# Another order of the units in the rounds of the RWKV-7 scan

## The chip, the core and the metric

The kernel runs on one core of a Trainium2 chip. The metric is the device time of one execution in microseconds (us), the median of the runs. A core has a matrix engine (TensorE, PE in the profile; PEld is its weight load), a vector engine (VectorE, DVE), a scalar engine (ScalarE, ACT), a general engine (GpSimd, POOL) and a queue engine (SyncE, SP) from which this kernel issues its DMA transfers. Each engine works through its own instructions in the order in which they stand in the program; between engines they wait on semaphores. Matrix products accumulate in PSUM, all other tiles lie in SBUF.

## The reference, cut to what matters

The program is a backbone of four layers over 256 latent and 256 context tokens of width 1024: attention, RWKV-7 time mixing, pooling, attention, each followed by a squared-ReLU MLP. All is float32. The change lies in layer 1, in the recurrent scan, which runs in two directions over 16 heads of width 64, first over the context and then, from the state reached there, over the latent tokens:

```
def _wkv_scan(state0, r, decay, k, v, kk, a, reverse):
    xs = tuple(jnp.moveaxis(t.astype(jnp.float32), 1, 0) for t in (r, decay, k, v, kk, a))

    def step(state, inp):
        r_t, w_t, k_t, v_t, kk_t, a_t = inp
        sa = jnp.einsum("bhvk,bhk->bhv", state, kk_t)
        state = (state * w_t[:, :, None, :]
                 - sa[..., None] * (kk_t * a_t)[:, :, None, :]
                 + v_t[..., None] * k_t[:, :, None, :])
        return state, jnp.einsum("bhvk,bhk->bhv", state, r_t)

    state, ys = lax.scan(step, state0, xs, reverse=reverse)
    return state, jnp.moveaxis(ys, 0, 1)
```

## The kernel before

The scan is done in chunks of 64 tokens. Within a chunk, the recurrence is a triangular system: its matrix (L, from the Gram products of keys and decays) is inverted, and the outputs and the chunk's effect on the state are then matrix products. The work is cut into 16 *units*, one for each block of 128 channels (two heads, `cc` 0 to 7) and stream (`s` = 1 context, 0 latent). One unit holds four chunks, two directions and two heads. A unit passes through stages, each written as a Python generator that issues a step of the stage's instructions each time it is called:

- `a` (`front_a`, lines 938 to 979): decays, keys and rates of the unit; ScalarE's E and iL, VectorE's tw, cum and ta. Its first step holds the product of line 943 and kkn (line 945).
- `b` (`front_b`, 981 to 1006): first step the Gram inputs KB and AR (988, 990 on VectorE, 989, 991 on GpSimd), then two steps of Gram products (996) with their masks NG (1001), whose L is stored to DRAM (1003), last the load of its diagonal blocks N (1006).
- `z` (`base`, 1051 to 1088): inversion of the 16x16 diagonal blocks on VectorE, in five steps: three of small products and subtractions (1067, 1069; two, two and three pairs), one with 1074 to 1076, one with 1078 to 1080, which also sends the result through DRAM into the tiles XT and X (1084, 1087).
- `c` (`front_c`, 1008 to 1047): six steps; the third and the fourth are transposes of KB with the copy NG (1035, 1037).
- `k` (`mv`, 1093 to 1102): M V, the product of the masked Gram matrix and V (1098), copied to XR (1101).
- `l` (`levels`, 1104 to 1137): two levels that grow the inverse from 16 to 64. Four steps: product L X and Tm (1114, 1126); two products and the subtractions into XT and X (1114, 1134, 1136); product L X and Tm on ScalarE (1114, 1128); product and subtraction into XT (1134).
- `h` (`chunks`, 1139 to 1183): five steps; two with line 1147, the third with the products 1157 and the subtractions P and Rp (1163, 1164), the fourth 1171, the fifth 1180 and Q (1182).
- `x` (`chain`, 1185 to 1214): the state S from chunk to chunk. `f` (`finish_a`) and `g` (`norms`, with `gate`, 1255 to 1264): normalization, gate and output of a finished block.

The matrix products of `k`, `l` and `h` write PSUM tiles `inv`, of which there are two; a third one waits until the first has been read. The transposes and Gram products share two tiles `pre`.

The units are pipelined: round n issues steps of different units at once. Which unit a letter works on is n plus its entry in `AHEAD` (`l` and `k`, `h`: the next unit, `z` and `c`: two ahead, `b`: three), and the order of the letters in the second string of `STEPS` is the order of the steps in a round. This order is binding for TensorE and VectorE alone: `ordered` chains their instructions one behind the other. For ScalarE, GpSimd and the DMA queue a scheduler orders the instructions by its own estimate.

The 16 rounds come in three kinds, and the text calls them so. In *even* rounds n the chain starts a new block (context), in *odd* ones it works on the latent stream. In *gate* rounds, n = 4, 8 and 12, which are even, two finished blocks are normalized and gated on top (`G`; lines 1233 to 1263).

Of the kernel before, what the change touches and what calls it, by code (L numbers as in the profile page):

```python
# [20 lines left out]
class Kern:  # L21
# [1337 lines left out]
AHEAD = dict(l=1, k=1, x=0, z=2, c=2, f=0, h=1, b=3, a=4, g=0, G=-1, A=3)  # L1359
STEPS = [[(z, AHEAD[z]) for z in order.split()] for order in (  # L1360
    "k l l l l z z z z z c c c c c c h h h h h A A b b b b a a",
    "G x c c x x c x x l x c l z k x G l A c A l x f c z z G h h b f a z G h z h h b G G f b b a g")]

ORDERED = 0
IN_ORDER = (mybir.EngineType.PE, mybir.EngineType.DVE)
# [162 lines left out]
```

## Time and profile before

| | us |
|---|---|
| median of 3 runs | 2509.22 (2504.28 to 2515.09) |
| profiled execution | 2503.11 |
| its span | 2501.3 |
| PE busy | 2324.9 (93%) |
| DVE busy | 1697.7 (68%) |
| ACT busy | 1110.1 (44%) |
| POOL busy | 324.9 (13%) |

The shares are averages over the whole program, most of which is MLP and projections. The scan's rounds lie between about 850 and 1320 us. In the profile a row of the timeline gives start and duration of one group of like instructions, and in brackets how long the engine stood idle before it and what it waited for.

### The profile page before, as it was taken

Reading aid. Unit: us, or ns where it says so; the run is one execution under the profiler, and the core shown is the slowest. Engines: PE = TensorE matmul, PEld = TensorE weight load, DVE = VectorE, ACT = ScalarE, POOL = GpSimd, SP = SyncE. Lnnn points to the kernel's source line nnn. Section 1 sums busy time; section 2 is a strip of 40 time slices with the busy share of each in tenths; the row PEclk is TensorE's granted clock in tenths of the full one; section 3 lists DMA queues with packets and bytes.
Section 4 is the critical chain, followed back from the end, with each engine's and each line's share of the span. In section 5 each row is a group of like instructions: output and inputs, shape, how many; then the busy total and the mean of one; then the engine's idle time right before and its main releaser. Section 6 shows DMA issues by size and latency. Waiting matters only on the chain. (4 is left out here: it accounts for less than half of the span.)

```text
span 2501.3 us, 41970 instructions
## 1 busy us (share of the span) xinstructions
PE 2324.9 (93%) x17082; PEld 1872.4 (75%) x17082; DVE 1697.7 (68%) x2845; ACT 1110.1 (44%) x2038; POOL 324.9 (13%) x414
## 2 busy tenths in 40 slices
PE   7999999999899987787889999999999999988999
PEld 5556888888677766565667888887888888866999
DVE  5777786673786566766666868655786673787555
ACT  4678523323564334443434532333523323576443
POOL 0100011101201222222210101110111100110110
PEclk9999999999899999999999999999999999998999
DMA  7431354553122322211132455532155452103453
GB/s 281 179 116 35 126 202 168 201 187 117 70 85 88 87 45 43 41 37 37 34 68 97 152 186 187 194 141 101 68 203 193 176 202 90 68 26 110 169 186 135
DMA packets 154833, 308.32 MB, mean 123 GB/s; under 512 B 107152, under 2 KB 111632, under 8 KB 122768
## 3 DMA queue, kind: packets, MB, share of 16 engines
q1 hardware_dynamic: 154640, 305.65, 35.8%
q8 instruction: 134, 2.20, 0.3%
q14 instruction: 59, 0.48, 0.1%
HBM read 294.58 MB, written 11.03 MB: 122 GB/s over the span
## 5 line engine op out<-in xcount | busy, mean ns | idle before, releaser
L252 DVE TENSOR_TENSOR wL<-wraw,wH 128x1024 fp32r<-128x1024 f32 (+1 forms) x364 | 408.2, 1124 | 288.1 <-ACT wH L251 287.5
L251 ACT CAST wH<-wraw 128x1024 fp32r<-128x1024 f32 (+1 forms) x364 | 342.1, 943 | 455.4 <-PE mm L262 432.3
L262 PE MATMUL mm<-hH,wL 128*128 128x512 f32 (+1 forms) x1296 | 471.4, 364 | 3.7 <-DVE wL L252 3.6
L262 PE MATMUL mm<-hH,wH 128*128 128x512 f32 (+1 forms) x1296 | 471.5, 364 | 2.6 <-ACT wH L251 2.4
L262 PE MATMUL mm<-hL,wH 128*128 128x512 f32 (+1 forms) x1296 | 466.5, 360 | 0.0
L262 PE MATMUL mm<-uH,wH 128*128 128x512 f32 (+1 forms) x1072 | 380.6, 355 | 0.0
L262 PE MATMUL mm<-uL,wH 128*128 128x512 f32 (+1 forms) x1072 | 379.4, 355 | 0.4 <-DVE uL L398 0.2
L262 PE MATMUL mm<-uH,wL 128*128 128x512 f32 (+1 forms) x1072 | 379.5, 354 | 0.0
L202 DVE SCALAR_TENSOR_TENSOR acc<-wraw,sc_sb,acc 128x2048 f32<-128x2048 f32 x126 | 300.4, 2404 | 25.1 <-DMA wraw<-in_w_mod 19.6
L394 POOL TENSOR_TENSOR usq<-relu 128x512 f32<-128x512 f32 (+1 forms) x128 | 146.3, 1144 | 1239.6 <-ACT relu L392 1237.1
L262 PEld LDWEIGHTS mm<-hH,wH 128*128 128x128 f32 x1296 | 245.4, 189 | 56.3 <-ACT wH L251 12.3
L262 PEld LDWEIGHTS mm<-hH,wL 128*128 128x128 f32 x1296 | 245.7, 190 | 43.8 <-DVE wL L252 6.2
L262 PEld LDWEIGHTS mm<-hL,wH 128*128 128x128 f32 x1296 | 245.6, 190 | 36.6 <-issue 1.1
L262 PEld LDWEIGHTS mm<-uL,wH 128*128 128x128 f32 x1072 | 202.3, 189 | 29.3 <-DVE uL L398 1.2
L262 PEld LDWEIGHTS mm<-uH,wL 128*128 128x128 f32 x1072 | 202.7, 189 | 28.4
L262 PEld LDWEIGHTS mm<-uH,wH 128*128 128x128 f32 x1072 | 202.7, 189 | 28.1
L341 DVE SCALAR_TENSOR_TENSOR x<-mm,mod,x 128x256 f32<-128x256 f32 x272 | 122.0, 479 | 146.1 <-PE mm L262 146.0
L392 ACT ACTIVATE relu<-mm 128x512 f32<-128x512 f32 (+1 forms) x128 | 69.2, 544 | 283.1 <-PE mm L262 279.4
L273 PE MATMUL mm<-hH,wH 128*128 128x256 f32 (+1 forms) x248 | 79.4, 323 | 17.5 <-ACT hH L323 10.0
L397 ACT CAST uH<-usq 128x512 fp32r<-128x512 f32 (+1 forms) x128 | 72.5, 568 | 47.9 <-POOL usq L394 47.9
L398 DVE TENSOR_TENSOR uL<-usq,uH 128x512 fp32r<-128x512 f32 (+1 forms) x128 | 80.5, 630 | 10.4 <-ACT uH L397 9.5
L273 PE MATMUL mm<-hH,wL 128*128 128x256 f32 (+1 forms) x248 | 78.1, 317 | 3.4 <-DVE wL L252 3.4
(344 smaller groups left out, 3697.1 us busy)
## 6 DMA issues: line engine op xcount, KB each, us to landing
wraw<-in_w_mod SPq DMA_DIRECT2D x96, 1024.0 KB, 4.9
wraw<-in_w_in SPq DMA_DIRECT2D x64, 1024.0 KB, 5.9
wraw<-in_w_out SPq DMA_DIRECT2D x64, 1024.0 KB, 5.0
wraw<-in_w_qk SPq DMA_DIRECT2D x10, 1024.0 KB, 4.8
wraw<-in_w_rkv SPq DMA_DIRECT2D x9, 1024.0 KB, 4.8
wraw<-in_w_ao SPq DMA_DIRECT2D x16, 512.0 KB, 4.0
Ls<-NG SPq DMA_DIRECT2D x32, 128.0 KB, 2.7
XT<-Xs SPq DMA_DIRECT2D x32, 128.0 KB, 3.1
```

Source lines behind the costliest of these rows:

```text
L202: nc.vector.scalar_tensor_tensor(acc, raw, self.sc[:, k, s:s + 1], acc, op0=ALU.mult, op1=ALU.add)
L251: nc.scalar.copy(h[:, sl], raw[:, sl])
L252: nc.vector.tensor_sub(l[:, sl], raw[:, sl], h[:, sl].bitcast(F32))
L262: self.nc.tensor.matmul(ps, lhsT=a[:, k], rhs=b, start=(n == 0), stop=(n == 3 * nk - 1))
L273: self.nc.tensor.matmul(ps[:, lo:hi], lhsT=a[:, k], rhs=b, start=(k == z == 0), stop=(k == nk - 1 and z == 2))
L341: self.nc.vector.scalar_tensor_tensor(self.x[o][:, a:b], ps, G[:, o, s:s + 1], self.x[o][:, a:b], op0=ALU.mult, op1=ALU.add)
L392: nc.scalar.activation(r[:, :n], ps[:, :n], AF.Relu)
L394: nc.gpsimd.tensor_mul(u2[:, :n], r[:, :n], r[:, :n])
L397: nc.scalar.copy(uH[:, :n], u2[:, :n])
L398: nc.vector.tensor_sub(uL[:, :n], u2[:, :n], uH[:, :n].bitcast(F32))
```

## The change

Only the string of a round in `STEPS` is another. The same steps are issued for the same units, in another order:

```
 AHEAD = dict(l=1, k=1, x=0, z=2, c=2, f=0, h=1, b=3, a=4, g=0, G=-1, A=3)
 STEPS = [[(z, AHEAD[z]) for z in order.split()] for order in (
     "k l l l l z z z z z c c c c c c h h h h h A A b b b b a a",
-    "G x c c x x c x x l x c l z k x G l A c A l x f c z z G h h b f a z G h z h h b G G f b b a g")]
+    "G x c c x x c x x c l x k l z z x G l A c A l x f c z z G h h f G h b a h z h b G G f b b a g")]
```

TensorE, the first half of a round, here an even one (`inv<-X,NG` is the first product of a level, `inv<-XT,Tm_6465` and `inv<-Tm_6465,XT` the second pair, `pre<-c_base,KB` the KB transposes, `inv<-VU,NG` is M V):

```order
 L1211 MATMUL yps<-Rp,S 64x64 x4
 L1201 MATMUL chain<-S,P 64x64 x4
+L1035 MATMUL pre<-c_base,KB 128x128 x4
 L1114 MATMUL inv<-X,NG 64x64 x16
 L1211 MATMUL yps<-Rp,S 64x64 x4
-L1035 MATMUL pre<-c_base,KB 128x128 x4
+L1098 MATMUL inv<-VU,NG 64x64 x16
 L1114 MATMUL inv<-XT,Tm_6465 64x64 x16
 L1114 MATMUL inv<-Tm_6465,XT 64x64 x16
-L1098 MATMUL inv<-VU,NG 64x64 x16
 L1201 MATMUL chain<-S,P 64x64 x4
```

The KB transposes move ahead of the first level product, and M V comes between the first product and the second pair.

VectorE, behind the subtractions of the first level in an even round (the rows of lines 1067 and 1069 are inversion steps; S and tw follow):

```order
 L1067 TENSOR_TENSOR tb<-Nb,Zb 64x24
 L1069 TENSOR_TENSOR Zb<-Zb,tb 64x2x6x2
+L1067 TENSOR_TENSOR tb<-Nb,Zb 64x30
+L1069 TENSOR_TENSOR Zb<-Zb,tb 64x2x5x3
+L1067 TENSOR_TENSOR tb<-Nb,Zb 64x32
+L1069 TENSOR_TENSOR Zb<-Zb,tb 64x2x4x4
 L1206 SCALAR_TENSOR_TENSOR S<-chain,lam,Q 128x64 x2
 L960 TENSOR_SCALAR tw<-tw 128x512
```

Two more pairs of the inversion's second step now stand in front of S; they are taken out of a place behind the second XT subtraction and line 1047, where the three pairs of the third step stay.

VectorE, further on in the same round (P and Rp of the `h` stage; KB, AR are Gram inputs, kkn belongs to the `a` stage; 1078 is the last inversion step):

```order
 L1163 TENSOR_TENSOR P<-c_rwkvB,inv 128x256
 L1164 TENSOR_TENSOR Rp<-AR,inv 128x256
+L988 TENSOR_TENSOR KB<-ta,iL 128x4x64
+L990 TENSOR_TENSOR AR<-kkn,E 128x4x64
+L988 TENSOR_TENSOR KB<-ta,iL 128x4x64
+L990 TENSOR_TENSOR AR<-kkn,E 128x4x64
+L945 SCALAR_TENSOR_TENSOR kkn<-kvr,vecs_sb,pre 128x256
 L1078 TENSOR_TENSOR tb<-Zb,tc 64x512
 L1079 TENSOR_REDUCE Zb<-tb 64x8x8
```

KB, AR and kkn stood ahead of line 1074 and now stand behind P and Rp, in front of the last inversion step. On TensorE, the product of line 943 moves behind that of line 1157.

On the engines that the scheduler orders, two things are different in a round: in odd rounds ScalarE has Tm (1128) and XR (1043) ahead of E (966), as it already had in even ones, and GpSimd has ks (1015) ahead of KB (989). The DMA queue keeps its order but for gate rounds, where the store of the first half of L (1003) now stands ahead of the reads of XT and X (1087).

## Rows read from the trace of the kernel before

**Rows 1.** The page of the kernel before: its first line, span and instructions.

```profile
span 2501.3 us, 41970 instructions
```

**Rows 2.** Waits, 850:1320 us: total us, times, longest.

```profile
PE inv L1180 <- DVE Rp L1164: 40.4, 13, 5.8
```

**Rows 3.** Stretches, odd and even round: busy us by engine, then granted clock, DMA.

```profile
1033.00:1061.00 28.00, 22.32 (x440) 17.93 (x438) 18.55 (x51) 11.62 (x29) 6.86 (x13) 1.00 0.22 42
...
1061.00:1090.00 29.00, 24.14 (x449) 19.71 (x445) 19.95 (x53) 10.94 (x27) 6.73 (x12) 0.94 0.20 38
```

**Rows 4.** Timeline of TensorE, an even round: start us, duration us; idle before.

```profile
1060.78 1.15 PE L1114 MATMUL inv<-X,NG 64*64 64x64 f32 x32 [0.64 <-DMA X<-Xs]
...
1062.09 0.66 PE L1035 MATMUL pre<-c_base,KB 128*128 128x128 f32 x4
...
1062.68 1.15 PE L1114 MATMUL inv<-XT,Tm 64*64 64x64 f32 x32
...
1065.29 0.97 PE L1098 MATMUL inv<-VU,NG 64*64 64x64 f32 x26 [0.52 <-DVE XT L1134]
...
1078.56 1.95 PE L1180 MATMUL inv<-VU,NG 128*64 128x64 f32 x32 [3.05 <-DVE Rp L1164]
```

**Rows 5.** Timeline of VectorE, the same even round.

```profile
1066.57 0.48 DVE L1206 SCALAR_TENSOR_TENSOR S<-chain,lam,Q 128x64 f32<-128x64 f32 x2 [0.20 <-PE chain L1201]
...
1069.20 0.42 DVE L1134 TENSOR_TENSOR XT<-XT,inv 128x256 f32<-128x256 f32 x1
...
1070.84 0.17 DVE L1067 TENSOR_TENSOR tb<-Nb,Zb 64x30 f32<-64x30 f32 x1
...
1073.05 0.18 DVE L1067 TENSOR_TENSOR tb<-Nb,Zb 64x30 f32<-64x30 f32 x1
...
1074.20 0.41 DVE L988 TENSOR_TENSOR KB<-ta,iL 128x256 f32<-128x256 f32 x1
...
1076.12 0.20 DVE L1074 COPY Zb<-Zb 64x64 f32<-64x64 f32 x1
...
1079.00 0.68 DVE L1078 TENSOR_TENSOR tb<-Zb,tc 64x512 f32<-64x512 f32 x1
...
1080.72 0.68 DVE L1182 TENSOR_TENSOR Q<-inv,lam 128x512 f32<-128x512 f32 x1
...
1082.38 1.29 DVE L1001 TENSOR_TENSOR NG<-pre,c_rwkvB 128x512 f32<-128x512 f32 x2 [0.99 <-PE pre L996]
```

**Rows 6.** Timeline of GpSimd, the same even round.

```profile
1070.86 1.43 POOL L989 TENSOR_TENSOR KB<-key,iL 128x256 f32<-128x256 f32 x2
...
1072.25 0.72 POOL L1015 TENSOR_TENSOR ks<-key 128x256 f32<-128x256 f32 x1
```

**Rows 7.** Timeline of the DMA queue (SPq), the same even round: issues.

```profile
1086.13 1.30 SPq L1087 DMA_DIRECT2D X<-Xs  x2
```

**Rows 8.** Timeline of TensorE, the odd round behind it.

```profile
1090.00 1.15 PE L1114 MATMUL inv<-X,NG 64*64 64x64 f32 x32 [0.64 <-DMA X<-Xs]
...
1098.21 1.15 PE L1114 MATMUL inv<-XT,Tm 64*64 64x64 f32 x32 [1.21 <-ACT Tm L1128]
...
1107.63 1.15 PE L1180 MATMUL inv<-VU,NG 128*64 128x64 f32 x32 [1.93 <-DVE Rp L1164]
```

**Rows 9.** Timeline of VectorE, the same odd round.

```profile
1099.40 0.42 DVE L1134 TENSOR_TENSOR XT<-XT,inv 128x256 f32<-128x256 f32 x1 [1.69 <-PE inv L1114]
```

**Rows 10.** Timeline of TensorE, a gate round.

```profile
994.61 0.66 PE L1035 MATMUL pre<-c_base,KB 128*128 128x128 f32 x4 [2.01 <-ACT ta L956]
...
1017.06 1.98 PE L1180 MATMUL inv<-VU,NG 128*64 128x64 f32 x32 [5.75 <-DVE Rp L1164]
```

**Rows 11.** Timeline of VectorE, the same gate round.

```profile
1017.50 0.89 DVE L1078 TENSOR_TENSOR tb<-Zb,tc 64x512 f32<-64x512 f32 x1
...
1023.72 0.69 DVE L1260 TENSOR_TENSOR yc<-yc,ssum 128x512 f32<-128x512 f32 x1 [1.51 <-ACT ssum L1259]
```

**Rows 12.** Timeline of GpSimd, the same gate round.

```profile
1016.58 2.95 POOL L1251 TENSOR_TENSOR yc<-yc,kvr 128x512 f32<-128x512 f32 x2 [3.43 <-ACT yc L1250]
```

More of the change, by code (lines that the diff above doesn't have):

```diff
@@ L1361 @@
     "k l l l l z z z z z c c c c c c h h h h h A A b b b b a a",
-    "G x c c x x c x x l x c l z k x G l A c A l x f c z z G h h b f a z G h z h h b G G f b b a g")]
+    "G x c c x x c x x c l x k l z z x G l A c A l x f c z z G h h f G h b a h z h b G G f b b a g")]
 ORDERED = 0
```

## The prediction

> **What bounds the kernel now.** I read the page first for the span, then the waits of the stretch in which the change works (the recurrent scan, about 850 to 1320 us), and then the timeline of its engines, iteration by iteration. The profiled execution took 2503.11 us for a span of 2501.3 us [rows 1], so 1.8 us lie around the span; the median of the runs shown is 2509.22 us, 6.1 us above that execution. Sums below are made against the profiled execution, and the difference is then set against the median.
>
> The scan is a loop of 16 rounds of some 28 us. Three kinds come in turn: even rounds, odd rounds, and every fourth round a gate round (even, with the output gate of a finished pair of chunks). In the waits the largest stop of TensorE is the product of line 1180, which waits for the R subtraction on VectorE: 40.4 us in 13 rounds [rows 2]. By the timelines these are 4 even rounds with 3.05 us, 6 odd ones with 1.93 and 3 gate rounds with 5.2 to 5.8; one of each is shown [rows 4, 8, 10]. What goes on meanwhile is seen in the VectorE rows of an even round [rows 5]: from the second XT subtraction (1069.20) to Q (1080.72) it works nearly without a stop. TensorE waits, but VectorE is what it waits for. So a wait on TensorE that goes is only worth what VectorE then does earlier for the next round.
>
> What carries a round into the next is a loop: Gram mask NG on VectorE, which ends at 1083.67 [rows 5]; behind it on the DMA queue the reads of X [rows 7]; these land 6.3 us after the mask, and the first level product of the next round waits for them, at 1090.00 with 0.64 us idle [rows 8], at 1060.78 the same [rows 4]. I therefore follow one number per round: when the first NG mask starts, counted from the first level product. Gate rounds have another entry and a longer tail, see below.
>
> **The change, part by part (even round, first level product at 1060.78).**
> 1. *M V ahead of the second level product, KB transposes ahead of the first.* Before, the product ran 1.31 us with the yps products behind it, then the KB transposes 0.59 (1062.09 to 1062.68), then the second level pair [rows 4]. After, M V (0.97) stands there in place of the transposes: the pair starts 0.39 later, and so does the XT subtraction behind it. M V's old place (0.52 wait and 0.97 work) becomes a wait for the X subtraction, of about the same length, so nothing is lost or won there. The transposes now fill the DMA wait in front of the first product: 0.59 into 0.3 to 1.3 us. I take 0.1 lost on average, between 0 and 0.3.
> 2. *Two more inversion steps (four small VectorE instructions) behind the level subtractions.* Before, they ran from 1070.84 to 1073.05, 2.21 us, beside GpSimd's KB and ks work (1070.86 to 1072.97); six like them right behind took 1.15 us with GpSimd done [rows 5, 6]. In the new place GpSimd has no such work in this round, and I take 4 x 0.20 = 0.80. They delay what follows: S (which no longer waits its 0.20), tw, cum, ta and the second XT subtraction. That comes at 1069.20 + 0.39 + 0.80 - 0.20 = 1070.2, 1.0 later, and E on ScalarE, GpSimd's AR and KB, and the yf addition are as late.
> 3. *What then falls beside GpSimd.* The next six inversion instructions start at 1071.9. GpSimd, as late as E, is then at ks (0.72, now ahead of KB) and KB (1.43) and done at about 1074.1 [rows 6]. I take three of the six stretched to the ends of GpSimd's pieces and three at full speed: done at 1074.75, 0.55 later than before (1074.20).
> 4. *P and R in front of the Gram inputs.* Four KB and AR products and kkn, 1.92 us (1074.20 to 1076.12) move behind P and R [rows 5]. R comes 1.92 - 0.55 = 1.4 earlier, and line 1180 waits 1.7 instead of 3.05. In the trace the product after the long wait took 1.95 us, against 1.15 in an odd round after a wait of 1.93 [rows 4, 8], and the mean granted clock of the even round is 0.94 where that of an odd one is 1.00 [rows 3]. With a wait no longer than the odd one's I expect the 2.4 GHz level to be kept. The Gram product then follows line 1180 with at most 0.2 for KB and AR.
> 5. *The sum on VectorE.* From the end of the six small ones to Q it is the same set of instructions, 6.52 us (1074.20 to 1080.72), in another order: Q starts 0.55 later. But then 0.99 us of wait for the Gram product goes [rows 5]. NG: 0.55 - 0.99 = -0.44. With the 0.1 of part 1, -0.35 per even round. Ends: -1.0 if the six small ones are not stretched at all, +0.1 if all are held to GpSimd's end.
>
> *Odd round after an even one.* The parts are the same. In addition ScalarE now runs the Tm product ahead of E, so the 1.21 us wait of the last level product goes [rows 8]; VectorE idled 1.69 us before the second XT subtraction [rows 9], which hides parts 1 and 2 (0.39 + 0.80) and leaves it 0.5 earlier. Against that stand three stretched small instructions where there was one, and no wait before NG to win back. I take 0; -0.5 to +0.6.
>
> *Gate round.* Here the first product starts on another path: ScalarE's table load and the work behind it, for which TensorE waits 2.01 us [rows 10]. That work starts behind the yvar product, which in the odd round before follows line 1180 and so moves up by about 1.3; half of this, 0.7, reaches the first level product, with the KB transposes done before it. The second XT subtraction comes 0.3 later (+0.39 + 0.80 - 0.20 - 0.7). The small instructions end 0.8 earlier: 2.2 of them have left this place, two of the six that stay are stretched by some 0.55 each. P and R come 0.8 + 1.92 = 2.7 earlier, and line 1180, which waits 5.75 us and then takes 1.98 [rows 10], with them. Q and NG gain less, about 1.1, since KB, AR and kkn stand ahead of them now. But the gate behind NG waits 1.51 us for TensorE's gate product [rows 11], which follows line 1180, so that this wait goes too: 1.1 + 1.5 = 2.6. What may be lost: GpSimd's two yc additions, 2.95 us [rows 12], now run beside KB and AR. I take -2.5 for the round, between -4 and -0.5.
>
> *Odd round after a gate one.* There is no DMA wait before the first product, so the transposes' 0.59 is paid in full: +0.6, between 0 and +1.
>
> Sum: even 4 x -0.35 = -1.4; odd 4 x 0; gate 3 x -2.5 = -7.5; odd after gate 3 x +0.6 = +1.8: -7 us. All the low ends give -18, all the high ends +4.
>
> How much two engines hinder each other is the disputed size. The row shows a VectorE instruction beside GpSimd's yc addition with 0.89 us [rows 11] and, without it, 0.68 in an even round [rows 5]: stretched, not stopped for the 1.47 of an addition. The Trainium skill ("SBUF — State Buffer", Who interferes with whom) says that a VectorE instruction with two SBUF inputs and a GpSimd one that reads SBUF exclude each other for the whole instruction, whoever starts first. By that rule the KB and AR products of the gate round would stand still until the additions end. The trace agrees with it in the even round, where the small instructions end with GpSimd's pieces, and not in the 0.89.
>
> **The rivals.**
> - *KB and AR held up in the gate round.* Both additions (2.95 us, [rows 12]) must end before the second of the four products runs: 1.0 more in each of 3 rounds: -7 + 3 = -4 us, 2505. For it: the small instructions of the even round end where GpSimd's pieces end. Against: the 0.89. This is the result of the rule quoted above.
> - *TensorE is the bound.* Then the wait before line 1180 is the price itself: 6 x 1.2, 4 x 1.4 and 3 x 2.5 less, and as much again from the low clock and from the 1.21 us: about -26 us, 2483. For it: 40.4 us of wait in one place. Against: VectorE works through the same stretch.
> - *Slower: the Gram inputs become the last.* KB and AR stand behind P and R now. If the Gram product must wait for the whole 1.92 us of them, the 0.99 us before NG stays, so the 0.55 of part 3 is paid, and with it the 0.59 of the transposes where ScalarE's VU copies free their buffer too late for the DMA wait: 1.1 us in 12 rounds, +13 us, 2522. It decides from the point where line 996 waits over 1 us for VectorE. For it: in the trace KB and AR were always done long before the product. Against: line 1180 itself, at its 1.15 us, covers the first two of the four (0.41 each).
> - *No change of the period.* X's landing stays where it is, because the queue of small transfers and not NG sets it: 0, 2509. Against: the read of X is issued right behind NG's store.
>
> **How the numbers follow.** Forecast -7 us: 2509.2 - 7 = 2502 us, chance 0.5. Gate products held up (2505) 0.13, TensorE the bound (2483) 0.15, slower (2522) 0.12, no change 0.10. About 0.5%, 12.5 us, is what a measurement of this kernel can tell from no change. Faster by more: the TensorE rival and the forecast's low end (0.18 of its 0.5): 0.33. Slower: 0.13. Between: 0.54. Range: from 2487, near the TensorE case and below the sum of the low ends, to 2514, the high ends and the scatter of the runs shown (2504 to 2515).
>
> **What would show it.** Right: in even rounds line 1180 waits about 1.7 us and runs 1.15 us, the wait before NG is gone, the small instructions behind kvr are still stretched, those behind X are not; odd rounds lose the 1.21 us wait and keep their length; gate rounds are 2 to 3 us shorter. Wrong: line 996 waits for KB or AR; the first level product waits for ScalarE; even rounds shorter by over 1 us (then VectorE was not the bound); gate rounds as long as before.

## The result and the profile after

The changed kernel takes 2522.98 us (median of 8 runs, 2520.22 to 2531.84) beside 2509.64 of the kernel before: the ratio is 1.0059, 95% interval 1.0041 to 1.0077. It is slower, by 13 us in the medians and 15 by the ratio; the forecast was 7 us faster. Its profiled execution took 2520.22 us; the page gives its span:

```profile
span 2518.4 us, 41974 instructions
```

The span is 17.1 us longer than before [rows 1]. The profiled execution of before lies 6.5 us below its median and that of the changed kernel 2.8, so a difference between these two traces comes out some 4 us too large. In the table, a round is counted from one first Tm subtraction (line 1126) to the next; each row is worked out from the 15 starts of one trace. *Plain* rounds are those which are neither gate rounds nor directly ahead of one.

| us | 8 plain rounds, mean | 3 rounds ahead of a gate round, sum | gate rounds 4, 8, 12 | all 14 |
|---|---|---|---|---|
| before | 28.03 | 85.8 | 37.4, 37.4, 36.7 | 421.5 |
| after | 29.33 | 89.4 | 38.4, 38.2, 41.0 | 441.7 |

The scan carries all of it: +20.2 us. The granted clock of TensorE (the third figure from the right in these windows, which give us busy by engine) fell over its whole length, from 0.96 before to 0.89 after:

```profile
850.00:1320.00 470.00, 376.92 (x6845) 299.32 (x6845) 312.50 (x805) 193.86 (x434) 106.33 (x182) 0.96 0.22 42
```

```profile
850.00:1320.00 470.00, 391.18 (x6509) 300.85 (x6509) 313.38 (x791) 191.26 (x422) 105.52 (x181) 0.89 0.21 41
```

The waits of TensorE in it (as in [rows 2]: total us, times, longest):

```profile
PE pre L996 <- DVE NG L1001: 23.8, 10, 2.4
PE inv L1147 <- DVE XT L1134: 15.1, 14, 3.2
...
PE pre L996 <- DVE AR L990: 6.2, 13, 1.5
...
PE inv L1180 <- DVE Rp L1164: 5.1, 6, 2.8
```

The 40.4 us in front of line 1180 have shrunk to 5.1. In their place stands a wait in front of the *second* Gram product of a unit, 2.38 us in 10 rounds: it needs the two `pre` tiles that the first product filled, and so the first NG mask. TensorE in round 6, the even round that [rows 4] show of before:

```profile
1070.97 1.15 PE L1114 MATMUL inv<-X,NG 64*64 64x64 f32 x32
...
1086.82 1.15 PE L1180 MATMUL inv<-VU,NG 128*64 128x64 f32 x32 [0.21 <-DVE Rp L1164]
1088.15 1.16 PE L996 MATMUL pre<-AR,KB 64*128 64x128 f32 x16 [0.18 <-DVE AR L990]
1089.24 0.70 PE L1228 MATMUL pre<-yf,c_base 128*128 128x256 f32 x2
1092.32 1.55 PE L996 MATMUL pre<-AR,KB 64*128 64x128 f32 x15 [2.38 <-DVE NG L1001]
...
1099.27 1.11 PE L1035 MATMUL pre<-c_base,KB 128*128 128x128 f32 x4
...
1101.90 1.15 PE L1114 MATMUL inv<-X,NG 64*64 64x64 f32 x32
```

The KB transposes ahead of the last row take 1.11 us, against 0.66 before [rows 4]. The windows of this round say why:

```profile
1071.00:1092.00 21.00, 16.61 (x373) 13.69 (x372) 16.12 (x43) 7.22 (x17) 5.31 (x9) 1.00 0.06 10
...
1094.00:1102.00 8.00, 7.64 (x61) 5.48 (x62) 2.92 (x9) 4.44 (x10) 1.48 (x4) 0.57 0.54 107
```

In the 8 us behind the new wait TensorE stands at its 1.2 GHz level for most of the time and is busy in 7.64 us of 8. The same round of the kernel before:

```profile
1078.00:1083.00 5.00, 4.42 (x50) 3.81 (x50) 3.94 (x10) 0.00 (x0) 0.00 (x0) 0.66 0.20 21
1083.00:1090.00 7.00, 5.73 (x73) 4.18 (x73) 3.78 (x11) 4.11 (x11) 1.78 (x4) 1.00 0.55 118
```

There the low clock lay on line 1180 and the first Gram product, and the way to the next first level product ran at 1.00. VectorE in round 6 after, to be held against [rows 5]:

```profile
1079.95 0.41 DVE L1134 TENSOR_TENSOR XT<-XT,inv 128x256 f32<-128x256 f32 x1
...
1083.09 0.64 DVE L1067 TENSOR_TENSOR tb<-Nb,Zb 64x24 f32<-64x24 f32 x1
...
1084.38 0.20 DVE L1074 COPY Zb<-Zb 64x64 f32<-64x64 f32 x1
...
1087.26 0.41 DVE L988 TENSOR_TENSOR KB<-ta,iL 128x256 f32<-128x256 f32 x1
...
1090.90 0.67 DVE L1182 TENSOR_TENSOR Q<-inv,lam 128x512 f32<-128x512 f32 x1
1091.50 1.27 DVE L1001 TENSOR_TENSOR NG<-pre,c_rwkvB 128x512 f32<-128x512 f32 x2
...
1097.30 0.48 DVE L1206 SCALAR_TENSOR_TENSOR S<-chain,lam,Q 128x64 f32<-128x64 f32 x2 [2.20 <-PE chain L1201]
```

The first mask starts 20.53 us behind the first level product (1070.97 to 1091.50), where it was 21.60 (1060.78 to 1082.38): 1.07 earlier. From the mask to the next first level product it is 10.40 us instead of 7.62: 2.78 later. That is the loss of this round, 1.71 us, and it lies behind the point to which the prediction counted.

### The profile page after: what moved, and what is told of

It reads as the page before. It is cut to its first block, busy times and chain, and to the rows that moved or that the text cites. A ratio compares the mean times of both kernels' runs of the same rounds, so it can differ in the third digit from the quotient of the medians.

```text
span 2518.4 us, 41974 instructions
## 1 busy us (share of the span) xinstructions
PE 2351.2 (93%) x17082; PEld 1885.1 (75%) x17082; DVE 1704.1 (68%) x2845; ACT 1112.7 (44%) x2038; POOL 325.4 (13%) x414
## 5 line engine op out<-in xcount | busy, mean ns | idle before, releaser
L996 PE MATMUL pre<-AR,KB 64*128 64x128 f32 x512 | 51.9, 325 | 34.1 <-DVE NG L1001 23.8
```

The source lines that it names most:

```text
L996: self.in_turn([nc.tensor.matmul(flat(pg[hh][:, q]), lhsT=flat(KB[rows(hh), dd, q]), rhs=AR[rows(hh), q, :, g(dd)], start=True, stop=True) ...
```

## Experiments

Two theories. **T1**: the 2.38 us gap lets TensorE fall to 1.2 GHz, and the slow stretch now lies on the entry of the next round, where TensorE is the bound. **T2**: VectorE's new order makes the second Gram product late, and the clock is a bystander. The strings below are the part of the round that differs; "..." stands for what is equal.

**The parts alone.** Transposes and M V alone:

```
-... c c x x c x x l x c l z k x G ...
+... c c x x c x x c l x k l z x G ...
```

> Only the KB transposes ahead of the first level product and M V between the level products; inversion steps and P, R stay where they were. Theory T1 (a gap of 2.4 us between the two Gram products lets TensorE fall to the 1.2 GHz level, and the slow stretch then lies on the entry of the next round): no such gap arises here, the second Gram product waits 0.2 to 0.3 us as before, 2509 us within 4. Theory T2 (KB, AR, kkn and the last inversion step in VectorE's order delay the second Gram product, and the clock is a bystander): the same, 2509. Rival T3 (the transposes and M V, not the P and R subtractions, carry the loss): 2520 us, with the first level product waiting for nothing and later by 0.6 to 1 us in each round.

Measured: 2514.51 us, ratio 1.0020 (1.0006 to 1.0033), 1.5 us above the range of T1 and T2. No new wait between the Gram products. The plain rounds are as before (28.28 on average); the rounds ahead of a gate round and the gate rounds are longer (96.6 and 117.3 in sum, against 85.8 and 111.4). A small loss, half of what T3 wanted.

The inversion's second step alone:

```
-... l x c l z k x G ...   f c z z G h h b f a z G h z h h b ...
+... l x c l z z k x G ... f c z G h h b f a z G h z h h b ...
```

> Only the inversion's second step moved behind the first level's subtractions. T1 and T2: P and R come up to 1.4 us earlier, the wait of line 1180 falls from 3.05 to about 2 us in even rounds, no new gap between the Gram products (0.2 to 0.3 us): 2503 to 2509 us. T3: the same.

Measured: 2507.16 us, ratio 0.9987 (0.9971 to 1.0002); the wait of line 1180 falls to at most 2.7 us. As expected.

P and R in front of the Gram inputs alone:

```
-... f c z z G h h b f a z G h z h h b ...
+... f c z z G h h f z G h b a h z h b ...
```

> Only P and R in front of KB, AR and kkn (the inversion's steps at their old places). T1 and T2: the second Gram product waits 2 to 2.5 us for the NG mask as in the changed kernel, and the kernel is slower than before, 2516 to 2524 us; by T1 with a granted clock of 0.5 in the 6 to 10 us behind that wait. T3: no loss, 2509 us or less.

Measured: 2526.03 us, ratio 1.0064 (1.0049 to 1.0079), the whole loss and 2 us more than the expected range. Its trace has the wait and the low clock behind it (TensorE, then a window):

```profile
1095.32 2.37 PE L996 MATMUL pre<-AR,KB 64*128 64x128 f32 x15 [2.38 <-DVE NG L1001]
...
1102.99 1.11 PE L1035 MATMUL pre<-c_base,KB 128*128 128x128 f32 x4
```

```profile
1094.00:1104.00 10.00, 8.68 (x56) 6.32 (x56) 4.40 (x10) 3.14 (x8) 1.29 (x3) 0.55 0.49 93
```

Both theories allow that; the next ones tell them apart.

**The gap filled.** The changed kernel, with the first Gram product issued three times over:

```
-  for q in range(4) for hh in range(2)])
+  for q in range(4) for hh in range(2) for _ in range((FILLER, 1)[dd])])
...
+FILLER = 3
```

> The changed kernel with the first Gram product of each unit issued three times over (the same values written again), so that TensorE works through the 2.38 us in which it waited for the NG mask; VectorE's order and work are the same. T1: the granted clock stays near 1.00 through the second Gram product and the entry of the next round, the first level product comes 2 to 3 us earlier behind the mask, and 10 rounds give back 15 to 25 us: 2498 to 2508 us. T2: the mask is no earlier and the added products are in the way: 2523 to 2530 us.

Measured: 2517.48 us, ratio 1.0020 (1.0004 to 1.0036), outside both ranges. The plain rounds do what T1 says, 27.32 us on average. Round 6:

```profile
1069.43 1.15 PE L1114 MATMUL inv<-X,NG 64*64 64x64 f32 x32 [0.33 <-DMA X<-Xs]
...
1086.23 3.25 PE L996 MATMUL pre<-AR,KB 64*128 64x128 f32 x48 [0.18 <-DVE AR L990]
...
1090.40 1.55 PE L996 MATMUL pre<-AR,KB 64*128 64x128 f32 x15 [0.30 <-DVE NG L1001]
...
1097.06 1.15 PE L1114 MATMUL inv<-X,NG 64*64 64x64 f32 x32
```

```profile
1092.00:1098.00 6.00, 5.64 (x93) 4.28 (x92) 3.00 (x9) 4.55 (x11) 1.91 (x5) 1.00 0.61 134
```

VectorE's order is that of the changed kernel, TensorE has 2.1 us more to do, the clock stays at 1.00, and the entry takes 6.66 us from the second Gram product (1090.40) instead of 9.58 (1092.32 to 1101.90). But in gate rounds the gate's own products stand in the gap and the filler lies on the path: those take 41.6, 43.4 and 42.8 us. Hence the same without rounds 4, 8 and 12 (the line added there makes the line numbers behind it one higher, as in the other runs that add lines):

```
+  for _ in range(1 if dd or self.it in (4, 8, 12) else 3)])
```

> The changed kernel with the first Gram product issued three times over, but not in rounds 4, 8 and 12, where the products of the gate already stand between the two Gram products and the added ones lay on the path (4.87 us at a granted clock of 0.5 in the run with the filler in all rounds). T1: rounds 1 to 3, 6, 7, 10 and 11 at 27.6 us as with the filler in all rounds, gate rounds as in the changed kernel: 2517.5 less 3 x 3 to 4 us, 2503 to 2509. T2: 2515 to 2523.

Measured: 2512.39 us, ratio 1.0005 (0.9992 to 1.0017): against 1.0059 the filler gives back 0.54%, 13.6 us, nearly the whole loss. T2 is out. The time is 3 us above T1's range: gate rounds take 119.4 us in sum and the rounds ahead of them 91.9, against 117.7 and 89.4 in the changed kernel. Round 8 takes 42.8 us without filler of its own, so the filler was not all that made it long.

A second trace of the changed kernel, from the runs side by side below, says the same without any filler. Its rounds 5 and 6 both have the gap; then TensorE:

```profile
1062.10 2.36 PE L996 MATMUL pre<-AR,KB 64*128 64x128 f32 x15 [2.38 <-DVE NG L1001]
...
1071.86 1.15 PE L1114 MATMUL inv<-X,NG 64*64 64x64 f32 x32
...
1093.05 1.55 PE L996 MATMUL pre<-AR,KB 64*128 64x128 f32 x15 [2.38 <-DVE NG L1001]
...
1099.73 1.15 PE L1114 MATMUL inv<-X,NG 64*64 64x64 f32 x32
```

```profile
1064.00:1072.00 8.00, 8.00 (x54) 5.29 (x52) 2.63 (x7) 4.48 (x11) 1.86 (x4) 0.51 0.65 130
1095.00:1101.00 6.00, 5.71 (x106) 4.60 (x108) 2.72 (x10) 4.68 (x11) 1.78 (x4) 1.00 0.57 126
```

In round 5 the clock falls behind the gap and the entry takes 9.76 us, in round 6 it holds and the entry takes 6.68; the rounds take 30.45 and 27.88. In the first trace it is the other way round: 27.27 and 30.93. So the low clock costs about 3 us where it falls, and the gap by itself does not.

**The mask earlier instead.** In the changed kernel, the last inversion step behind the first mask:

```
-... h h f G h b a h z h b G G ...
+... h h f G h b a h h b z G G ...
```

> The changed kernel with the last inversion step (lines 1078 to 1080, 1.7 us on VectorE) behind the first NG mask instead of ahead of P's Gram stage; nothing is added. The mask comes 1.7 us earlier, so that the second Gram product waits 0.2 to 0.8 us instead of 2.38; the results of the inversion go out through DRAM 2 us later against the mask and the first level product waits for X again. T1: the clock is kept, the round is set by X: 2505 to 2516 us, with most of the low-clock stretches behind line 996 gone. T2: the mask is what sets the round, so the whole 1.7 us come back in 10 rounds: 2500 to 2507 us.

Measured: 2527.22 us, ratio 1.0063 (1.0049 to 1.0078); both ranges missed. The gap shrinks to at most 0.9 us (0.68 ahead of the row below), but X, which that step sends through DRAM, becomes the last, and the clock falls on its wait instead:

```profile
PE inv L1114 <- DMA X<-Xs: 20.6, 10, 3.6
```

```profile
1109.99 1.98 PE L1114 MATMUL inv<-X,NG 64*64 64x64 f32 x32 [3.10 <-DMA X<-Xs]
```

**Was the low clock free before?** The kernel before with filler ahead of line 1180, in even rounds without a gate:

```
-  for q in range(4) for hh in range(2) for dd in range(2)])
+  for q in range(4) for hh in range(2) for dd in range(2)
+  for _ in range(1 if self.it % 2 or self.it in (4, 8, 12) else 3)])
```

> The kernel before with the product of line 1157 issued three times over in even rounds without a gate, 2.6 us of TensorE work ahead of the 3.05 us in which line 1180 waits for VectorE. T1 in the form that the low clock costs nothing where VectorE is what TensorE waits for: the clock stays near 1.00 around line 1180 in those rounds, and the time stays within 3 us of before, 2506 to 2512. If low clock cost the same wherever it falls: 4 to 5 rounds times 1 to 2 us less, 2500 to 2504 us.

Measured: 2508.20 us, ratio 0.9990 (0.9977 to 1.0002), in the range for "costs nothing". Round 6 of its trace (line 1180 is 1181 here):

```profile
1064.88 1.15 PE L1114 MATMUL inv<-X,NG 64*64 64x64 f32 x32 [0.45 <-DMA X<-Xs]
...
1083.10 1.10 PE L1181 MATMUL inv<-VU,NG 128*64 128x64 f32 x32
...
1092.84 1.15 PE L1114 MATMUL inv<-X,NG 64*64 64x64 f32 x32 [0.28 <-DMA X<-Xs]
```

It takes 27.96 us against 29.22 before (1060.78 to 1090.00). But that is the round that gained most: the four with filler (0, 2, 6, 10) take 28.68, 28.03, 27.96 and 28.90 us, before 28.39, 27.80, 29.22 and 29.47, 1.3 us less in sum. So the low clock cost little at the old place, against some 3 us a round at the new one; whether by its place or by its length (0.66 over 5 us before, 0.57 over 8 after) no run tells apart.

**Without the transposes and M V.** Inversion steps and P, R moved, the rest as before, without filler and with it outside gate rounds:

```
-... c c x x c x x c l x k l z z x G ...
+... c c x x c x x l x c l z z k x G ...
```

> The change without its first part: inversion steps and P, R moved, KB transposes and M V where they stood in the kernel before, no filler. T1: the wait of 2.4 us between the Gram products and the low clock behind it are there, so that it lies 8 to 14 us above the same order with the filler: 2514 to 2522 us. T2: the filler cannot matter in this order either: 2507 within 3.

> The filler outside gate rounds as above, and of the change only the inversion steps and the P and R subtractions; the KB transposes and M V stand where they stood in the kernel before. The run with the transposes and M V alone was 5 us slower than before. T1 with that part as a loss of its own: 2500 to 2506 us, below both kernels. T2: 2512 to 2523.

Measured: 2514.55 us, ratio 1.0007 (0.9997 to 1.0018), and with filler 2506.75 us, 0.9985 (0.9972 to 0.9999). The second beats both kernels, by a hair against before, and lies 0.75 us above T1's range; its plain rounds take 27.17 us. The filler is worth 0.22% here, less than the 8 to 14 us that T1 wanted, though the trace has 24.6 us of the gap's wait in 11 rounds. The traces show a part of the reason: with the filler the 14 rounds take 417.0 us instead of 440.9, but round 0 begins at 887.0 us instead of 878.2. The filler also stands in the three units whose Gram products come ahead of round 0; that it costs the time there was not tested.

**The change without P and R** (`h h b f a G h z h h b` in place of `h h f G h b a h z h b`):

> The change without P and R in front of the Gram inputs: transposes, M V and inversion steps moved. Both theories hold the P and R subtractions for the cause of the gap: no wait over 1 us between the Gram products, and the sum of the two parts alone (+5 and -2 us): 2510 to 2516 us. Rival: the three parts only cost together: 2509 or less.

Measured: 2512.99 us, ratio 1.0003 (0.9990 to 1.0015), no gap over 0.9 us: no loss clear of the noise without P and R. The sum that was expected (+3 us) and the rival (none) cannot be told apart by this interval.

**Filler in gate rounds as well**, where line 1147 waits, on top of the best version:

```
+  for _ in range(4 if self.it in (4, 8, 12) else 1):
       nc.tensor.matmul(pb[:, :T], lhsT=c["meanH"], rhs=ks, start=True, stop=True)
```

> The version without the first part and with the filler outside gate rounds, and in gate rounds the product of line 1046 issued four times, 2.1 us of work into the 1.8 to 2.4 us in which line 1147 waits for the second XT subtraction. T1: line 1147 runs 1.96 us there instead of 2.8 to 3.5, but P and R wait for VectorE and not for it, so that little follows: 2501 to 2507 us. If low clock cost the same wherever it falls: 3 rounds times 1.5 us less than without it, 2500 to 2503 us.

Measured: 2516.97 us, ratio 1.0009 (0.9995 to 1.0022): worse than without, and 10 us above the expected range. Line 1147 does run at full clock, but the clock falls later in the round, on the gate's products (windows of round 4; the version without this filler behind it):

```profile
1012.00:1024.00 12.00, 8.14 (x138) 6.16 (x136) 11.16 (x24) 5.34 (x12) 6.16 (x8) 1.00 0.01 1
1024.00:1040.00 16.00, 13.88 (x44) 6.52 (x44) 8.16 (x15) 3.05 (x6) 1.43 (x5) 0.50 0.30 58
```

```profile
1012.00:1018.00 6.00, 5.54 (x106) 3.92 (x102) 5.90 (x13) 2.92 (x6) 1.60 (x2) 0.94 0.01 3
1018.00:1024.00 6.00, 4.53 (x21) 2.59 (x20) 5.82 (x10) 0.00 (x0) 1.19 (x2) 0.72 0.10 11
1024.00:1034.00 10.00, 8.03 (x65) 4.47 (x64) 5.50 (x12) 5.42 (x13) 1.71 (x4) 1.00 0.52 112
```

The low clock comes later and lasts longer, on the products of the gate: gate rounds of 41.7, 41.8 and 39.0 us instead of 36.5, 38.9 and 37.3.

**Side by side.** Why 1.0059 with the transposes and M V, and 1.0007 without?

> The changed kernel once more, beside the order without its first part. If the first part costs of itself once P and R are moved (T1 with a second cause): 2519 to 2526 us, 6 to 10 us above its neighbour. If the numbers differ only from one set of runs to another: within 3 us of it, about 2515 to 2520.

> The change without its first part once more: 2512 to 2517 us by the first reading; within 3 us of the changed kernel by the second.

> First and third part, the inversion steps at their old places. If the first part costs of itself beside the moved P and R: 2530 to 2536 us, above the 2526 of P and R alone. If it does not: 2523 to 2528 us, as P and R alone. That is the base from which the inversion steps take 5 to 14 us.

Measured on one chip: 2521.37 us, ratio 1.0050 (1.0033 to 1.0068); 2512.76, 1.0013 (1.0000 to 1.0025); 2525.67, 1.0061 (1.0039 to 1.0083). The difference is real, 8.6 us beside moved P, R and inversion steps; beside P and R alone the first part costs nothing that can be measured (1.0061 against 1.0064). So the parts do not add up. Two traces of either kernel differ by 5.6 us in gate round 12: 41.0 and 40.9 with the first part, 35.3 and 35.3 without. With it, the clock is low through all of the gate's products there (TensorE, the changed kernel, then the one without the first part):

```profile
1277.65 1.15 PE L1180 MATMUL inv<-VU,NG 128*64 128x64 f32 x32 [2.78 <-DVE Rp L1164]
...
1284.29 2.07 PE L1258 MATMUL pre<-hid_g,wg 32*128 32x512 f32 x2
...
1289.04 2.07 PE L1258 MATMUL pre<-hid_g,wg 32*128 32x512 f32 x2
```

```profile
1275.77 1.15 PE L1180 MATMUL inv<-VU,NG 128*64 128x64 f32 x32 [0.95 <-DVE Rp L1164]
...
1282.15 1.12 PE L1258 MATMUL pre<-hid_g,wg 32*128 32x512 f32 x2
...
1285.01 1.12 PE L1258 MATMUL pre<-hid_g,wg 32*128 32x512 f32 x2
```

But that does not place the 8.6 us, since other rounds are longer without the first part: all 14 take 441.7 and 442.8 us with it, 440.9 and 437.3 without. Where the difference arises, and why the clock of round 12 is kept in the one and not in the other, stays open.

## Why the prediction was wrong

The forecast was 2502 us, at most 2514; it took 2523. The step that failed is the measure to which all parts were added up, "one number per round: when the first NG mask starts", and with it the sentence of part 4, "I expect the 2.4 GHz level to be kept", which looked at line 1180 alone. In round 6 the mask came 1.07 us earlier, but the way from it to the next round took 2.78 us more, at a granted clock of 0.57 behind a wait that the forecast did not have; with that wait filled the kernel is 13.6 us faster.

- *Parts 1 to 3* hold in kind and not in size. The small steps behind X run at 0.16 to 0.18 us, three of the six behind kvr are stretched (0.64 to 0.77) and M V lies between the products. But the second XT subtraction comes 8.98 us behind the first level product (1079.95 less 1070.97), against 8.42 [rows 4, 5], where I had expected 1.0 more; and what follows the six small ones starts 13.41 us behind that product (1084.38 less 1070.97), against 13.42 (1074.20 less 1060.78), where I had expected 0.55 more. That term was nothing.
- *Part 4* was right on the duration of line 1180, 1.15 us; its wait fell to 0.21 us and not to 1.7. It did not follow TensorE's idle time further. That time did not all go: with KB, AR, kkn, the last inversion step and Q between P, R and the mask, it turned up behind the first Gram product.
- *Part 5* was too small on its own ground: the mask starts 1.07 us earlier, at the low end of -1.0, not 0.44: the 0.99 of wait in front of it is gone and the 0.55 of part 3 did not come. With the clock kept by the filler, a plain round is 0.67 us shorter than before (27.36 against 28.03). Up to the mask VectorE gained more than the forecast said; what the forecast left out comes behind the mask, where round 6 loses 2.78 us.
- *Odd rounds*: I took 0. The wait for Tm is gone as forecast (7.9 us in 7 waits before, none after). Rounds in which the clock happened to hold, as round 5 with 27.27 us against 27.71, are even shorter; where it fell they take 29.7 us or more (rounds 1, 9 and 11: 29.74, 30.41 and 29.74).
- *Gate rounds*: -2.5 was forecast, they came out at +1.0, +0.9 and +4.3. One trace of a gate round proves little: in the kernel before with filler in other rounds they take 41.6, 38.9 and 36.9 us, instead of 37.4, 37.4 and 36.7. Line 1180 in round 4 waits 0.89 us instead of 5.75 [rows 10], but the wait is handed on: KB and AR now meet GpSimd's yc additions [rows 12], and the first Gram product waits 1.47 us for AR. VectorE, then GpSimd, in round 4 after:

```profile
1025.09 0.63 DVE L988 TENSOR_TENSOR KB<-ta,iL 128x256 f32<-128x256 f32 x1
1025.64 1.48 DVE L990 TENSOR_TENSOR AR<-kkn,E 128x256 f32<-128x256 f32 x1
1027.05 0.41 DVE L988 TENSOR_TENSOR KB<-ta,iL 128x256 f32<-128x256 f32 x1
```

```profile
1024.16 2.68 POOL L1251 TENSOR_TENSOR yc<-yc,kvr 128x512 f32<-128x512 f32 x2 [5.26 <-ACT yc L1250]
```

AR takes 1.48 us instead of 0.41 and ends 0.28 behind the additions. This is the first rival's mechanism, at its price of about 1 us a round. The Trainium skill ("SBUF — State Buffer", Who interferes with whom) describes an exclusive hold; the row of AR agrees with it, but the 0.63 us of the first KB, which also runs beside an addition, do not look like a full hold, nor did the 0.89 us [rows 11] from which I weighed against it.
- *The rival "slower"* named the size, 2522, and its deciding point, line 996 over 1 us behind VectorE, but not the cause, so that its number is luck: the first Gram product waits 0.18 us for AR; it is the second one that waits, and the price is the clock behind it. "TensorE is the bound" is refuted as told: 35 us less wait in front of line 1180 brought no gain. Its price was not added up right either: the three terms come to 20.3 us, and as much again would be 41, not 26.

## What to carry to other kernels

Where another engine is the bound, moving a wait of TensorE need not remove its idle time; look for where it turns up, and then for what TensorE must do in the 7 to 10 us behind it, because that may run at half clock. A replay of the bounding engine has to be carried through to the start of the next round, not to a milestone in it. Filling a gap with repeated products is a cheap test of whether the clock is the cause, and here worth 0.5% of the program; check its trace as well, for here filler in another gap was followed by a longer low clock at a worse place.

## What was not expected of the hardware

- A gap of 2.38 us was followed by 7 to 10 us at 1.2 GHz in 8 of the 10 rounds that had it, and by none in rounds 5 and 10 (27.27 and 28.25 us). Behind a wait of 2.46 us for ta the transposes ran at full clock in one kernel (0.66 us, inversion step alone), and behind one of 2.48 us at the low one in another (1.11 us, transposes and M V alone).
- The Trainium skill ("TensorE: Matmul & The Clock Gate", Terms) puts the penalty of a throttled stretch at its length times the share of the clock withheld. For the 8 us window at 0.57 that gives, as an estimate by the Trainium skill's rule, 3.4 us; the trace agrees roughly, as the entry of that round takes 9.58 us and with the filler 6.66, 2.9 less.
- Work added in front of a slow stretch can bring the program forward (13.6 us, by fillers of 2.1 us in the rounds without a gate) or put it back (6 us by the ratios, by three fillers of 1.3 us), by where the clock falls next and for how long.
